# Seven block products instead of eight in the second feed-forward product of a decoder layer

## The chip, the core and the metric

The kernel runs on one core of one Trainium2 chip. The metric is the device time of one execution in microseconds. All operands are float32; matmuls read float32 that has been split into a high and a low part (type fp32r), three matmuls for one product: high x high, low x high, high x low.

## What is computed

The reference is one decoder layer on x of 512 positions and 1024 channels: an input projection into two token mixers, their merge and output projection, a layer norm, and the feed-forward part that the change touches:

```python
h = layer_norm(DEEPNORM_ALPHA * h + mix, ln1_g[l], ln1_b[l])
f = jnp.square(jax.nn.relu(h @ w_ff1[l])) @ w_ff2[l]      # w_ff1 1024 x 4096, w_ff2 4096 x 1024
h = layer_norm(DEEPNORM_ALPHA * h + f, ln2_g[l], ln2_b[l])
```

## The kernel before

The feed-forward part goes through the 4096 hidden channels in four quarters of 1024 (`for q in range(4)`, L890). In each, a first stage (FF1 here) makes the hidden activations of the quarter, and a second stage (FF2) multiplies them by the quarter's 1024 rows of w_ff2 and adds the product to the residual `hn`.

FF1 works on two column blocks n of 512 channels and uses the seven-product form of a 2 x 2 block product (Strassen's, in Winograd's variant): instead of eight products of half-size blocks it makes seven of sums of blocks, numbered p = 1, 2, 5, 6, 3, 7, 4. `ff1_product(n, p)` (L844) runs 24 matmuls of 256 columns with the weight blocks stationary. The sums of the activations (X, L778 to L822, L835) are made once. The sums of the weights are made by DMA: `du_chunks` (L211) loads three chunks for a block: U (two of the four weight blocks, in ring "raw"), V (one) and S (one, twice). `dma_add` (L207) is a DMA on the GpSimd (POOL) queue that adds one tile into another. `s13` (L239) adds U into S, both halves, before product 1 (it is the `pre` of that item); `du_item` (L221) adds S's first half into U's second after product 1's split, for product 6, and U's second half into V after product 2's split, for product 3. FF1's results are kept in small tiles (`small_t`, tag "bt", five buffers, L784), then put through relu and square, and split into `ah` and `al` by `rest` (L880), run behind the next product's matmuls.

FF2 is plain: `b_step` (L726) takes one row block k (128 hidden channels) of w_ff2 and runs 4 position tiles x 2 column halves x 3 matmuls of 512 columns, weights moving, activations stationary, into eight PSUM banks over eight k (L901). Then DVE adds the banks into `hn` (L908). The weights of FF2 come as row pairs (`rows_b`, L168, L263) through ring "raw". In the last quarter the stage is ordered by position tile, so that the last layer norm can start early (L913 to L920).

All weights pass through one `Stream` (L41): a list of chunks (DMA loads into rings of two buffers each, "raw", "V", "S") and a list of items. `ws.get()` returns the split of the next item and prepares the items up to two further on: it issues the loads that a ring has room for (a chunk's place is free when the last item of the chunk two before it has been made) and then the split, `split` (L142): a copy on ScalarE into `whi`, a subtraction on VectorE into `wlo`, three buffers each. Loads are issued by SyncE (SP, L80). `ffseq` (L245) holds the order of the FF1 items: in quarter 0 the two blocks are interleaved by hand, in the others the second block's product 1 comes seventh. The order in which an engine gets its instructions is that of a scheduler that the program goes through, mostly, but not always, the order of the code. `consts` (L719) loads the two vectors of a layer norm into a slab, for the last norm at the end of quarter 0 (L911). "slab" is a pool of eight tiles of 16 KB a partition. `norm_in` and `norm_out` (L739, L745) are the layer norm.

The functions printed below are those that the change touches.

Of the kernel before, what the change touches and what calls it, by code (L numbers as in the profile page):

```python
# [9 lines left out]
F32 = mybir.dt.float32  # L10
F32R = mybir.dt.float32r
# [89 lines left out]
def layer_kernel(ctx: ExitStack, tc: tile.TileContext, x, w_in, gm_ln_g, gm_ln_b, gm_w_s, gm_b_s,  # L101
# [109 lines left out]
    def du_chunks(src, k0, c0):  # L211


        def blk(n, k):
            return src[:, k0 + 4 * k:k0 + 4 * k + 4, c0 + 256 * n:c0 + 256 * n + 256]
        one, two = (lambda t: t[:, 0]), (lambda t: t[:, 1])
        return dict(U=ws.chunk("raw", [2, 4, 256], [(two, blk(0, 0)), (one, blk(1, 1))]),
                    V=ws.chunk("V", [4, 256], [((lambda t: t), blk(0, 1))]),
                    S=ws.chunk("S", [2, 4, 256], [(one, blk(1, 0)), (two, blk(1, 0))]))
# [25 lines left out]
    ffseq = []  # L245
    for q in range(4):
        du = [2 * q, 2 * q + 1]
        if q == 0:
            order = [(0, 1), (0, 2), (1, 1), (1, 2), (0, 5), (0, 6), (0, 3), (0, 7), (1, 5), (0, 4), (1, 6),
                     (1, 3), (1, 7), (1, 4)]  # L250
        else:
            order = [(0, 1), (0, 2), (0, 5), (0, 6), (0, 3), (0, 7), (1, 1), (0, 4), (1, 2), (1, 5), (1, 6),
                     (1, 3), (1, 7), (1, 4)]
        ffseq.append([(2 * q + i, p) for i, p in order])
        dus = {}
        for n, p in ffseq[q]:
            if n not in dus:
                dus[n] = du_chunks(w1v, 0, 512 * n)
# [467 lines left out]
    def b_step(banks, k, hi, lo, ah, al, start, stop, ts, es=(0, 1)):  # L726
        for t in ts:
            ts_ = slice(t * P, (t + 1) * P)
            for e in es:
                cs = slice(e * 512, (e + 1) * 512)  # L730
                ps = banks[2 * t + e]
                nc.tensor.matmul(ps, ah[:, k, ts_], hi[:, cs], start=start, stop=False)  # L732
                nc.tensor.matmul(ps, al[:, k, ts_], hi[:, cs], start=False, stop=False)  # L733
                nc.tensor.matmul(ps, ah[:, k, ts_], lo[:, cs], start=False, stop=stop)  # L734
# [89 lines left out]
    for t in range(4):  # L824
        for e in range(2):
            for k in range(2, 8):
                b_step(ob, k, *last[k - 2], mh, ml, False, k == 7, [t], [e])
# [11 lines left out]
    ah = slab("ah", [P, 8, S], F32R)  # L839
    al = slab("al", [P, 8, S], F32R)  # L840
# [3 lines left out]
    def ff1_product(n, p):  # L844
# [26 lines left out]
        if p == 4:  # L871
            t = small_t("b")
# [4 lines left out]
        c0 = 4 * (n % 2) + (2 if p in (4, 7) else 0)  # L877
        rows, cs = slice(c0, c0 + 2), slice(0, 256) if p in (2, 4) else slice(256, 512)

        def rest():  # L880
            if p != 4:
                nc.scalar.activation(t, t, AF.Relu, scale=-1.0 if p == 7 else 1.0)
            t3 = t.rearrange("p (k i) -> p k i", k=2)
            nc.scalar.activation(t, t, AF.Square)
            nc.scalar.activation(ah[:, rows, cs], t3, AF.Copy)
            nc.vector.tensor_sub(al[:, rows, cs], t3, ah[:, rows, cs].bitcast(F32))

        later.append(rest)

    for q in range(4):  # L890
# [7 lines left out]
        if q == 3:
            res["fh"] = slab("fh", [P, 4, D], F32R)
            res["fl"] = slab("fl", [P, 4, D], F32R)  # L900
        for k in range(8 if q < 3 else 2):  # L901
            hi, lo = ws.get()
            b_step(fb, k, hi, lo, ah, al, k == 0, k == 7, range(4))
        if q < 3:
            for t in range(4):
                for e in range(2):
                    cs = slice(e * 512, (e + 1) * 512)
                    nc.vector.scalar_tensor_tensor(hn[:, t, cs], hn[:, t, cs], ALPHA if q == 0 else 1.0,  # L908
                                                   fb[2 * t + e], op0=ALU.mult, op1=ALU.add)
            if q == 0:  # L910
                consts(ln2_g, ln2_b)  # L911
        else:
            last = [ws.get() for _ in range(6)]  # L913
            for t in range(4):
                for e in range(2):
                    for k in range(2, 8):
                        b_step(fb, k, *last[k - 2], ah, al, False, k == 7, [t], [e])
                    norm_in(t, e, fb, 1.0)
                norm_out(t, EPS, lambda cs: (nc.scalar if cs.start else nc.sync).dma_start(
                    out[t * P:(t + 1) * P, cs], hn[:, t, cs]))  # L920
# [30 lines left out]
```

## Time and profile before

| what | value |
|---|---|
| median of 3 runs | 903.93 us (902.53 to 905.6) |
| profiled execution, its own time | 902.12 us |
| its span, first to last instruction | 900.4 us |
| mean granted TensorE clock | 0.994 |
| busy: PE, DVE, ACT | 883.7, 494.2, 384.4 us |
| DMA | 110.10 MB, mean 122 GB/s |

PE is TensorE, DVE VectorE, ACT ScalarE, POOL GpSimd, SP SyncE, PEld TensorE's weight load, which runs beside the matmuls. A q behind an engine's name is its instruction queue. Busy time is the time in which an engine had an instruction running; matmuls overlap each other in the pipeline. In a table of instructions, "out<-in" names the program's tiles with buffer numbers left out, and "idle" is the time before an instruction in which its engine had nothing running, with what ended it.

### The profile page before, as it was taken

To read this page: it belongs to the slowest core of one execution; us is meant where nothing else is said; L and a number is where in the kernel's file an instruction comes from. 1 tells how busy PE (TensorE), PEld (TensorE's weight loads), DVE (VectorE), ACT (ScalarE), POOL (GpSimd) and SP (SyncE) were. 2 spreads that over 40 slices of the span, in tenths; PEclk is the share of its full clock that TensorE was granted. 3 is DMA by queue.
4 is the path that set the end of the run, shared out by engine and by line. 5 is a ranking of instruction groups with operands and counts; after the bars stand their busy time and mean duration, and the time that the engine had idled before them with its cause. 6 is when DMAs were issued, how large, how long until landed. Compare 5 with 4: busy or idle time off the path is not lost.

```text
span 900.4 us, 12170 instructions
## 1 busy us (share of the span) xinstructions
PE 883.7 (98%) x4864; PEld 762.1 (85%) x4864; DVE 494.2 (55%) x961; ACT 384.4 (43%) x668; POOL 31.0 (3%) x44
## 2 busy tenths in 40 slices
PE   8999999999999999999999998999999999999995
PEld 6888898988888888788788887988998899889984
DVE  3322745542237766667745589742563266346667
ACT  3522312342225566565533316751474167227700
POOL 1000000000000000000000011001100100010000
PEclk9999999999999999999999999899999999999999
DMA  7458510343232011311174653565664866374401
GB/s 233 122 166 244 163 40 25 96 140 94 94 94 77 18 47 48 94 48 48 47 270 152 182 122 71 171 204 140 130 197 141 193 150 188 127 170 110 141 24 70
DMA packets 71513, 110.10 MB, mean 122 GB/s; under 512 B 2656, under 2 KB 54688, under 8 KB 71456
## 3 DMA queue, kind: packets, MB, share of 16 engines
q1 hardware_dynamic: 62336, 85.04, 29.1%
q0 software_dynamic: 4608, 16.78, 9.8%
q10 hardware_dynamic: 4512, 7.50, 2.8%
q8 instruction: 38, 0.62, 0.3%
q14 instruction: 19, 0.16, 0.1%
HBM read 90.44 MB, written 2.10 MB: 103 GB/s over the span
## 4 chain that ended last, share of the span: by engine, by line
PE 97%; DVE 2%; ACT 1%; DMA 0%; issue 0%; DVEq 0%; SPq 0%; ACTq 0%
PE ps L133 13%; PE ps L135 12%; PE ps L134 12%; PE ps L732 8%; PE ps L734 8%; PE ps L733 8%; PE ps L862 6%; PE ps L860 6%; PE ps L863 6%; PE ps L656 2%; PE ps L406 2%; PE ps L407 2%; PE ps L451 2%; PE ps L408 2%; PE ps L671 1%; PE ps L673 1%
## 5 line engine op out<-in xcount | busy, mean ns | idle before, releaser
L151 DVE TENSOR_TENSOR wlo<-raw,whi 128x1024 fp32r<-128x1024 f32 (+3 forms) x131 | 152.8, 1168 | 222.6 <-ACT whi L150 222.4
L150 ACT ACTIVATE whi<-raw 128x1024 fp32r<-128x1024 f32 (+3 forms) x131 | 132.7, 1015 | 270.4 <-PE ps L134 114.9
L860 PE MATMUL ps<-x,whi 128*128 128x256 f32 x448 | 128.5, 287 | 2.9 <-ACT x L800 2.7
L862 PE MATMUL ps<-x,whi 128*128 128x256 f32 x448 | 128.0, 286 | 1.6 <-DVE x L801 1.6
L133 PE MATMUL ps<-xh,whi 128*128 128x512 f32 x320 | 128.8, 403 | 0.0
L863 PE MATMUL ps<-x,wlo 128*128 128x256 f32 x448 | 127.8, 285 | 0.0
L134 PE MATMUL ps<-xl,whi 128*128 128x512 f32 x320 | 125.2, 391 | 0.2 <-DVE xl L338 0.2
L135 PE MATMUL ps<-xh,wlo 128*128 128x512 f32 x320 | 125.2, 391 | 0.0
L860 PEld LDWEIGHTS ps<-x,whi 128*128 128x128 f32 x448 | 87.1, 194 | 5.1 <-ACT x L800 3.3
L862 PEld LDWEIGHTS ps<-x,whi 128*128 128x128 f32 x448 | 87.0, 194 | 2.2 <-DVE x L801 2.1
L732 PE MATMUL ps<-whi,ah 128*128 128x512 f32 x224 | 87.3, 391 | 0.0
L733 PE MATMUL ps<-whi,al 128*128 128x512 f32 x224 | 87.3, 390 | 0.0
L734 PE MATMUL ps<-wlo,ah 128*128 128x512 f32 x224 | 87.2, 389 | 0.0
L863 PEld LDWEIGHTS ps<-x,wlo 128*128 128x128 f32 x448 | 87.0, 194 | 0.0
L135 PEld LDWEIGHTS ps<-xh,wlo 128*128 128x128 f32 x320 | 60.1, 188 | 13.0
L134 PEld LDWEIGHTS ps<-xl,whi 128*128 128x128 f32 x320 | 60.3, 189 | 9.9 <-DVE xl L338 0.5
L133 PEld LDWEIGHTS ps<-xh,whi 128*128 128x128 f32 x320 | 60.2, 188 | 9.3
L615 ACT ACTIVATE PP<-PP,nm 128x512 f32<-128x512 f32 (+3 forms) x64 | 35.8, 559 | 35.5 <-DVE nm L609 35.2
L732 PEld LDWEIGHTS ps<-whi,ah 128*128 128x128 f32 x224 | 42.1, 188 | 9.3 <-ACT b L873 1.0
L734 PEld LDWEIGHTS ps<-wlo,ah 128*128 128x128 f32 x224 | 42.1, 188 | 8.8
L733 PEld LDWEIGHTS ps<-whi,al 128*128 128x128 f32 x224 | 42.1, 188 | 8.4
L660 DVE TENSOR_TENSOR ptl<-ps,pth 128x512 fp32r<-128x512 f32 (+1 forms) x48 | 31.7, 683 | 8.0 <-ACT pth L659 7.9
(205 smaller groups left out, 1529.0 us busy)
## 6 DMA issues: line engine op xcount, KB each, us to landing
raw<-in_w_in_dram SPq DMA_DIRECT2D x17, 1024.0 KB, 5.2
raw<-in_w_ff_dram SPq DMA_DIRECT2D x16, 1024.0 KB, 5.1
S<-in_w_ff_dram SPq DMA_DIRECT2D x16, 512.0 KB, 5.7
raw<-in_w_ff_dram SPq DMA_DIRECT2D x16, 512.0 KB, 4.8
S<-raw POOLq DMA_DIRECT2D x16, 512.0 KB, 5.9
raw<-in_w_in_dram SPq DMA_DIRECT2D x8, 512.0 KB, 3.7
raw<-in_w_proj_gm_dram SPq DMA_DIRECT2D x4, 1024.0 KB, 5.2
raw<-in_w_proj_nsa_dram SPq DMA_DIRECT2D x4, 1024.0 KB, 5.1
```

Of the source, the lines that this page charges most:

```text
L133: nc.tensor.matmul(ps, hi, mh, start=start, stop=False)
L134: nc.tensor.matmul(ps, hi, ml, start=False, stop=False)
L135: nc.tensor.matmul(ps, lo, mh, start=False, stop=stop)
L150: nc.scalar.activation(hi, r, AF.Copy)
L151: nc.vector.tensor_sub(lo, r, hi.bitcast(F32))
L615: nc.scalar.activation(t, t, AF.Exp, bias=nm[:, e, i:i + 1], scale=-1.0, accum_out=sm[:, e, i:i + 1])
L732: nc.tensor.matmul(ps, ah[:, k, ts_], hi[:, cs], start=start, stop=False)
L733: nc.tensor.matmul(ps, al[:, k, ts_], hi[:, cs], start=False, stop=False)
L734: nc.tensor.matmul(ps, ah[:, k, ts_], lo[:, cs], start=False, stop=stop)
L860: nc.tensor.matmul(o, hi[:, k, js], xh[:, k], start=opens and j == 0 and k == 0, stop=False, skip_group_check=True)
L862: nc.tensor.matmul(o, hi[:, k, js], xl[:, k], start=False, stop=False, skip_group_check=True)
L863: nc.tensor.matmul(o, lo[:, k, js], xh[:, k], start=False, stop=j == 1 and k == 3, skip_group_check=True)
```

## The change

In quarters 0 to 2, FF2 also uses the seven-product form. Its 2 x 2 blocks are: position halves of 256, hidden-channel halves of 512, and output-column halves of 512. The weight blocks are loaded and summed by the same three chunks and DMA adds (`ff2_blocks`, a quarter has two sets h, each half of the hidden channels of a block). The sums of the activations (Y) are made in `rest`, from the small tiles, by subtractions on VectorE, and split into new slabs y12, y56, y37 and the free half of x4; `ah` and `al` go. `ff2_product` runs, for each p in the order 1, 2, 6, 5, 7, 3, 4 and each of the two sets, 2 x 2 x 3 matmuls of 512 columns, weights moving; products that add into one output share their banks, and after each product VectorE adds or subtracts two banks into `hn`. Quarter 3 keeps the plain form, with the activations taken from Y1, Y2, Y5 and Y3. The load of the last norm's vectors moves to quarter 3. The "bt" ring has six buffers instead of five.

The core of the diff (`b_step` now asks a function for its activation tiles, which is left out here, as are the changed calls):

```diff
+    def ff2_blocks(q, h):
+        def blk(half, k):
+            k0 = 8 * q + 4 * k + 2 * h
+            return w2v[:, k0:k0 + 2, 512 * half:512 * half + 512]
+        return du_chunks([2, 512], blk)
...
-    ffseq = []
+    ffseq, FF2 = [], (1, 2, 6, 5, 7, 3, 4)
...
         if q < 3:
-            rows_b(w2v, list(range(8 * q, 8 * q + 8)), 0, 1024)
+            dus = [ff2_blocks(q, h) for h in range(2)]
+            for p in FF2:
+                for h in range(2):
+                    du_item(dus[h], p, s13(dus[h]) if p == 1 else None)
...
-    ah = slab("ah", [P, 8, S], F32R)
-    al = slab("al", [P, 8, S], F32R)
+    y12 = slab("y12", [P, 4, D], F32R)
+    y56 = slab("y56", [P, 4, D], F32R)
+    y37 = slab("y37", [P, 4, D], F32R)
+    Y = {p: (block(t, i), block(t, i + 1)) for p, (t, i) in
+         {1: (y12, 0), 2: (y12, 2), 5: (y56, 0), 6: (y56, 2), 3: (y37, 0), 7: (y37, 2), 4: (x4, 2)}.items()}
...
+        def y_split(c, t):
+            t3 = t.rearrange("p (k i) -> p k i", k=2)
+            nc.scalar.activation(Y[c][0][:, rows], t3, AF.Copy)
+            nc.vector.tensor_sub(Y[c][1][:, rows], t3, Y[c][0][:, rows].bitcast(F32))
 
         def rest():
             if p != 4:
                 nc.scalar.activation(t, t, AF.Relu, scale=-1.0 if p == 7 else 1.0)
-            t3 = t.rearrange("p (k i) -> p k i", k=2)
             nc.scalar.activation(t, t, AF.Square)
-            nc.scalar.activation(ah[:, rows, cs], t3, AF.Copy)
-            nc.vector.tensor_sub(al[:, rows, cs], t3, ah[:, rows, cs].bitcast(F32))
+            t11, t12, t22 = g[1], g.get(6), g.get(5)
+            plain = n // 2 == 3
+            if p == 2:
+                y_split(1, t)
+            elif p == 3:
+                if plain:
+                    y_split(5, t)
+                else:
+                    nc.vector.tensor_sub(t11, t11, t12)
+                    y_split(5, t11)
+            elif p == 7:
+                y_split(3, t)
+                if not plain:
+                    nc.vector.scalar_tensor_tensor(t11, t11, -1.0, t22, op0=ALU.mult, op1=ALU.subtract)
+                    y_split(6, t11)
+                    nc.vector.tensor_sub(t12, t22, t12)
+                    y_split(7, t12)
+            else:
+                y_split(2, t)
+                if not plain:
+                    nc.vector.scalar_tensor_tensor(t, t11, -1.0, t, op0=ALU.mult, op1=ALU.subtract)
+                    y_split(4, t)
...
+    def ff2_product(q, p):
+
+        where = {1: "A", 2: "B", 5: "C", 6: "A", 3: "C", 7: "A", 4: "A"}[p]
+        opens = p in (1, 2, 5)
+        if opens:
+            g2[where] = [bank(t) for t in {"A": "dd", "B": "aa", "C": "ac"}[where]]
+        for h in range(2):
+            hi, lo = ws.get()
+            for j in range(2):
+                js = slice(j * P, (j + 1) * P)
+                ps = g2[where][j]
+                for kk in range(2):
+                    yh, yl = (y[:, 2 * h + kk, js] for y in Y[p])
+                    nc.tensor.matmul(ps, yh, hi[:, kk], start=opens and h == 0 and kk == 0, stop=False,
+                                     skip_group_check=True)
+                    nc.tensor.matmul(ps, yl, hi[:, kk], start=False, stop=False, skip_group_check=True)
+                    nc.tensor.matmul(ps, yh, lo[:, kk], start=False, stop=h == 1 and kk == 1,
+                                     skip_group_check=True)
+        half, e, sign, first = {1: (0, 0, 1, 1), 2: (0, 0, 1, 0), 6: (1, 0, 1, 1), 5: (1, 1, -1, 1),
+                                7: (1, 1, -1, 0), 3: (1, 0, 1, 0), 4: (0, 1, -1, 1)}[p]
+        for j in range(2):
+            v = hn[:, 2 * half + j, e * 512:(e + 1) * 512]
+            nc.vector.scalar_tensor_tensor(v, v, ALPHA if q == 0 and first else 1.0, g2[where][j],
+                                           op0=ALU.mult, op1=ALU.add if sign > 0 else ALU.subtract)
...
+        if q < 3:
+            for p in FF2:
+                ff2_product(q, p)
+            continue
         fb = eight()
...
+        consts(ln2_g, ln2_b)
```

## Rows read from the trace of the kernel before

**Rows 1.** The page, part 4: the chain that ended last, by engine.

```profile
PE 97%; DVE 2%; ACT 1%; DMA 0%; issue 0%; DVEq 0%; SPq 0%; ACTq 0%
```

**Rows 2.** Windows: start:end, length, busy us (x instructions), clock, DMA share, GB/s.

```profile
core 0: us, PE busy (x) PEld busy (x) DVE busy (x) ACT busy (x) POOL busy (x), PEclk, DMA share, GB/s
593.20:636.50 43.30, 43.30 (x202) 36.12 (x203) 13.55 (x14) 12.04 (x14) 4.26 (x5) 1.00 0.59 152
636.50:677.40 40.90, 40.90 (x329) 40.00 (x327) 27.24 (x32) 28.19 (x39) 2.55 (x3) 1.00 0.61 169
```

**Rows 3.** Timeline of PE inside FF2: start us, duration us, instruction.

```profile
604.47 0.39 PE L732 MATMUL ps<-whi,ah 128*128 128x512 f32 x1
...
630.31 0.39 PE L732 MATMUL ps<-whi,ah 128*128 128x512 f32 x1
```

**Rows 4.** Groups by line and shape, window 593.2 to 677.4.

```profile
L151 DVE TENSOR_TENSOR wlo<-raw,whi 128x1024 fp32r<-128x1024 f32 x15 | 18.4, 1224 | 28.1 <-ACT whi L150 28.1
L150 ACT ACTIVATE whi<-raw 128x1024 fp32r<-128x1024 f32 x14 | 14.8, 1060 | 30.9 <-PE ps L733 23.2 <-PE ps L862 7.7
...
L908 DVE SCALAR_TENSOR_TENSOR hn<-hn,ps 128x512 f32<-128x512 f32 x8 | 5.0, 679 | 4.0 <-PE ps L734 4.0
```

**Rows 5.** Windows at the start of FF1 in quarter 0.

```profile
550.00:555.00 5.00, 5.00 (x44) 5.00 (x43) 4.96 (x13) 3.83 (x6) 0.26 (x1) 1.00 0.56 108
560.00:565.00 5.00, 2.08 (x8) 1.78 (x9) 5.00 (x9) 3.28 (x6) 0.00 (x0) 0.68 0.00 0
565.00:570.00 5.00, 5.00 (x30) 5.00 (x30) 4.62 (x7) 2.03 (x3) 0.00 (x0) 0.64 0.61 213
```

**Rows 6.** Timeline of PE there.

```profile
559.08 0.28 PE L863 MATMUL ps<-x,wlo 128*128 128x256 f32 x1
...
563.50 0.58 PE L862 MATMUL ps<-x,whi 128*128 128x256 f32 x1 [0.82 <-DVE x L801]
```

**Rows 7.** Waits of SP's queue: us in total, times, longest.

```profile
SPq L721 <- DVE T L820: 52.3, 1, 52.3
```

**Rows 8.** Timeline of DVE: the last two splits of w2 (rows 30, 31).

```profile
856.31 2.36 DVE L151 TENSOR_TENSOR wlo<-raw,whi 128x1024 fp32r<-128x1024 f32 x2 [0.35 <-ACT whi L150]
```

**Rows 9.** Line L732 on the kept w2 rows of quarter 3: ns min/median/max, first and last start.

```profile
L732 PE MATMUL ps<-fh,ah x32: 389/389/389, 858.5 to 889.1; 128*128 128x512 f32 x32
```

**Rows 10.** Timeline of SP's queue: the issue of one U, two halves.

```profile
613.59 0.93 SPq L80 DMA_DIRECT2D raw<-in_w_ff_dram  x2
```

**Rows 11.** Timeline of POOL: issues of DMA adds; in brackets idle time before, its end.

```profile
549.00 0.84 POOL L208 DMA_DIRECT2D raw<-S  x1 [2.44 <-DVE rs L315]
554.74 0.85 POOL L208 DMA_DIRECT2D V<-raw  x1 [4.90 <-DVE hn L764]
...
619.19 0.86 POOL L208 DMA_DIRECT2D S<-raw  x1 [0.57 <-DMA raw<-in_w_ff_dram]
...
630.61 1.12 POOL L208 DMA_DIRECT2D raw<-S  x1
640.60 0.85 POOL L208 DMA_DIRECT2D V<-raw  x1 [8.88 <-DMA raw<-S]
652.67 0.84 POOL L208 DMA_DIRECT2D raw<-S  x1 [11.21 <-DVE wlo L151]
660.64 0.86 POOL L208 DMA_DIRECT2D V<-raw  x1 [7.12 <-DMA raw<-S]
```

**Rows 12.** Timeline of ACT: the split of V that waited for its add.

```profile
665.33 1.06 ACT L150 ACTIVATE whi<-V 128x1024 fp32r<-128x1024 f32 x1 [0.88 <-DMA V<-raw]
```

**Rows 13.** DMA view, window 590 to 690; issues: KB each, median us to landing.

```profile
DMA packets 8377, 16.48 MB, mean 165 GB/s; under 512 B 398, under 2 KB 5694, under 8 KB 8371
...
S<-raw POOLq DMA_DIRECT2D x4, 512.0 KB, 5.2
```

**Rows 14.** The chain that ended last in order of time: start, us.

```profile
592.49 0.23 PE ps L732
593.18 0.33 PE ps L860
```

**Rows 15.** A window with an add and loads together.

```profile
652.00:657.00 5.00, 5.00 (x44) 5.00 (x43) 3.40 (x5) 3.88 (x5) 0.84 (x1) 1.00 1.04 288
```

More of the change, by code (lines that the diff above doesn't have):

```diff
@@ L209, in dma_add, with du_chunks, ff1_blocks, blk @@
                             accum_op=ALU.add)
-    def du_chunks(src, k0, c0):
-        def blk(n, k):
-            return src[:, k0 + 4 * k:k0 + 4 * k + 4, c0 + 256 * n:c0 + 256 * n + 256]
+    def du_chunks(shape, blk):
         one, two = (lambda t: t[:, 0]), (lambda t: t[:, 1])
-        return dict(U=ws.chunk("raw", [2, 4, 256], [(two, blk(0, 0)), (one, blk(1, 1))]),
-                    V=ws.chunk("V", [4, 256], [((lambda t: t), blk(0, 1))]),
-                    S=ws.chunk("S", [2, 4, 256], [(one, blk(1, 0)), (two, blk(1, 0))]))
+        return dict(U=ws.chunk("raw", [2] + shape, [(two, blk(0, 0)), (one, blk(1, 1))]),
+                    V=ws.chunk("V", shape, [((lambda t: t), blk(0, 1))]),
+                    S=ws.chunk("S", [2] + shape, [(one, blk(1, 0)), (two, blk(1, 0))]))
+    def ff1_blocks(n):
+        def blk(half, k):
+            c0 = 1024 * (n // 2) + 512 * half + 256 * (n % 2)
+            return w1v[:, 4 * k:4 * k + 4, c0:c0 + 256]
+        return du_chunks([4, 256], blk)
+    def ff2_blocks(q, h):
+        def blk(half, k):
+            k0 = 8 * q + 4 * k + 2 * h
+            return w2v[:, k0:k0 + 2, 512 * half:512 * half + 512]
+        return du_chunks([2, 512], blk)
     def du_item(d, p, pre=None):
@@ L724, in layer_kernel, with b_step @@
     consts(ln1_g, ln1_b)
-    def b_step(banks, k, hi, lo, ah, al, start, stop, ts, es=(0, 1)):
+    def b_step(banks, k, hi, lo, get, start, stop, ts, es=(0, 1)):
         for t in ts:
-            ts_ = slice(t * P, (t + 1) * P)
+            th, tl = get(k, t)
             for e in es:
@@ L731, in b_step @@
                 ps = banks[2 * t + e]
-                nc.tensor.matmul(ps, ah[:, k, ts_], hi[:, cs], start=start, stop=False)
-                nc.tensor.matmul(ps, al[:, k, ts_], hi[:, cs], start=False, stop=False)
-                nc.tensor.matmul(ps, ah[:, k, ts_], lo[:, cs], start=False, stop=stop)
+                nc.tensor.matmul(ps, th, hi[:, cs], start=start, stop=False)
+                nc.tensor.matmul(ps, tl, hi[:, cs], start=False, stop=False)
+                nc.tensor.matmul(ps, th, lo[:, cs], start=False, stop=stop)
     def eight():
@@ L767, in norm_out, with m_tile @@
                     emit(cs)
+    def m_tile(k, t):
+        return mh[:, k, t * P:(t + 1) * P], ml[:, k, t * P:(t + 1) * P]
     ob = eight()
@@ L771, in layer_kernel @@
         hi, lo = ws.get()
-        b_step(ob, k, hi, lo, mh, ml, k == 0, False, range(4))
+        b_step(ob, k, hi, lo, m_tile, k == 0, False, range(4))
     last = [ws.get() for _ in range(6)]
@@ L826, in layer_kernel @@
             for k in range(2, 8):
-                b_step(ob, k, *last[k - 2], mh, ml, False, k == 7, [t], [e])
+                b_step(ob, k, *last[k - 2], m_tile, False, k == 7, [t], [e])
             norm_in(t, e, ob, 2.0 * ALPHA)
@@ L890, in layer_kernel, with a_tile @@
+    def a_tile(k, t):
+        y = Y[{(0, 0): 1, (1, 0): 2, (0, 1): 5, (1, 1): 3}[k // 4, t // 2]]
+        ts_ = slice(t % 2 * P, t % 2 * P + P)
+        return y[0][:, k % 4, ts_], y[1][:, k % 4, ts_]
     for q in range(4):
@@ L896, in layer_kernel @@
             later.pop(0)()
+        if q < 3:
+            for p in FF2:
+                ff2_product(q, p)
+            continue
         fb = eight()
[L898 to L920, printed above, removed]
+        res["fh"] = slab("fh", [P, 4, D], F32R)
+        res["fl"] = slab("fl", [P, 4, D], F32R)
+        consts(ln2_g, ln2_b)
+        for k in range(2):
+            b_step(fb, k, *ws.get(), a_tile, k == 0, False, range(4))
+        last = [ws.get() for _ in range(6)]
+        for t in range(4):
+            for e in range(2):
+                for k in range(2, 8):
+                    b_step(fb, k, *last[k - 2], a_tile, False, k == 7, [t], [e])
+                norm_in(t, e, fb, 1.0)
+            norm_out(t, EPS, lambda cs: (nc.scalar if cs.start else nc.sync).dma_start(
+                out[t * P:(t + 1) * P, cs], hn[:, t, cs]))
 _INS = ['x', 'w_in', 'gm_ln_g', 'gm_ln_b', 'gm_w_s', 'gm_b_s', 'cmp_pe_k', 'cmp_w1_k', 'cmp_w2_k',
```

10 lines of the change are left out of this document (5 added, 5 removed).

## The prediction

> **What bounds the kernel now.** First the page's chain: TensorE (PE) carries 97% of what ended last [rows 1]. So the time is the sum of PE's instructions, and an edit is worth the PE time it removes, less the new time in which PE waits. The table of windows cuts the changed part into stages: a second-product stage ("FF2") of 43.3 us, then a first-product stage ("FF1") of 40.9 us, PE busy all through both, VectorE (DVE) and ScalarE (ACT) at about a third in FF2 and two thirds in FF1, the DMA engines at 0.6 [rows 2]. Last the timelines: a matmul's duration (0.39 us) overlaps the next one, so its price is the step from start to start. Between the two starts shown lie 114 matmuls of 512 columns in 25.84 us: 0.2267 us each [rows 3]. FF1 and FF2 of a quarter take 84.2 us [rows 2]; the 192 FF2 matmuls are 43.5, so 336 FF1 matmuls share 40.7: 0.121 us each, and one FF1 item (24 matmuls) is 2.91 us.
>
> **What is removed.** FF2 of a quarter had 8 x 4 x 2 x 3 = 192 matmuls. Afterwards it has 7 products x 2 halves x 2 row tiles x 2 k x 3 = 168, of the same shape (stationary 128x128 activations, 512 weight columns moving), so the same step holds. Three quarters lose 24 each: 72 x 0.2267 = 16.3 us. That is the whole possible gain: 902.1 (the profiled execution; its span is 900.4) becomes 885.8. The median of the runs, 903.9, lies 1.8 above the profiled one, and I add that at the end.
>
> **Work beside PE.** An FF2 quarter gets 14 weight splits instead of 8 (1.06 us ACT, 1.22 DVE) and 14 bank drains instead of 8 (0.68 DVE) [rows 4]: DVE 26.6 us and ACT 14.8 us, beside 168 x 0.2267 = 38.1 us of PE. Hidden. FF1 of quarters 0 to 2 gets, for its two blocks, 14 activation splits instead of 8 and 8 combinations: 6 copies on ACT, each half as wide as a weight split's 1.06, and 14 DVE instructions of the drain's shape (0.68) [rows 4]. On the windows' times: ACT at most 28.2 + 6.4 = 34.6, DVE 27.2 + 9.5 = 36.7 of 40.9 us [rows 2]. Hidden, but DVE stands at 90%. The nearest rows for a full DVE are the start of FF1 in quarter 0, where DVE was busy in 4.96 to 5.00 of 5.00 us and PE had one matmul between 559.08 and 563.50, 4.4 us [rows 5, 6]. Bounds 0 to 4.4 us a quarter; I take 0, since 10% is left and whi/wlo have three buffers, so that a split may be nearly two items late. A gain is excluded: nothing is taken from these engines.
>
> The drains don't hold PE: products 1, 6, 7, 4 share banks, and between each two lies another product of 5.4 us against 2 x 0.68 of draining. Y of product 1 comes early in FF1, and Y2, the last of the first ones, is wanted 5.4 us after FF2 begins. y37, a ninth slab, can reuse hraw, free before product 7. The sixth bt buffer only adds room.
>
> The constants move from quarter 0 to quarter 3. Before, SP (the queue that issues loads) stood 52.3 us with them at its head, weight loads behind [rows 7]; no PE wait follows from it, so freeing it gains 0. In quarter 3 their two issues wait for a slab that FF1's last products free, and their 1 MB passes ahead of the last w2 rows. The nearest price is U's 1 MB, 5.6 us from issue to landing (below). Those rows are split by 856.31 + 2.36 = 858.7 [rows 8], while the row-26 matmuls begin at 858.5 and rows 30 and 31 come 12 matmuls (2.7 us) later [rows 9]: 2.5 us to spare. 0 taken, as the loads overlap; up to 3.1 in the range.
>
> **The chain that decides.** A new set of weight blocks needs DMAs in a row: U loads; S += U; U1 += S0 (for product 6); V += U1 (for product 3). Before, w2 rows lay between two FF1 stages, used unchanged, and gave this chain time. Now every item uses it. Prices: U, issued at 613.59, lets its second S add go at 619.19, 5.6 later [rows 10, 11]; an S add lands in 5.2 [rows 13]. U1 += S0, from its issue to the start of the V add that waits for it, takes at most 5.7 us (549.00 to 554.74), 8.0 beside S loads (652.67 to 660.64), and 10.0 with two other adds ahead (630.61 to 640.60) [rows 11]; the V add 4.7, to the split at 665.33 [rows 12]. After landing, a split costs some 2.0 us before PE can run through.
>
> *Entering FF1 after FF2* (0 = its first matmul). The raw buffer is freed by the split of product 4, half 0, which starts four items of 2.72 ahead, at -10.9, and ends near -8.4. U: -2.8; product 1 is in time. S0: +2.4. U1: +8.1 to +12.4, so product 6 can run from 10.1 to 14.4. The written order wants it as fourth item, at 8.7. But the order on PE is not the written one: in the chain an FF2 matmul (L732, 592.49) stands ahead of the last FF1 product (L860, 593.18) [rows 14]. The program is ordered by readiness, so I expect products 1 and 2 of the second block, whose U and V are there, to go ahead of product 6: it is then wanted at 14.5, not late. Product 3 is wanted at 17.4 and has V at 12.8 to 17.1, split at 14.8 to 19.1. Late by 0 to 1.7 us; I take 1.7, the row with two adds ahead, since the second block's S adds fall here. Three times: 5.1 us.
>
> *Entering FF2.* U of half 1 is freed by the split of the last FF1 product, starting at -8.7: S0 at +4.5, U1 at +10.2 to +14.5, product 6 of half 1 ready at 12.2 to 16.5, wanted as sixth item at 13.6. Late 0 to 2.9; with 8.0 us, the row beside S loads, 0.9. Three times: 2.7 us.
>
> **Sum:** 16.3 - 5.1 - 2.7 = 8.5 us; 902.1 - 8.5 = 893.6, and with 1.8 **895.4**.
>
> How far can these latencies be trusted? 100 us of the trace move 16.48 MB [rows 13], a quarter 13.9. Eight further adds of 0.52 MB and 1.05 MB more loads make 19.1 MB in 79 us. The window with an add and loads together moved 288 GB/s [rows 15], at which this is 66 us: 84% of the quarter, so queues will form. The Trainium skill (Trainium Kernel Development and Optimization, Key Constraints) says that DMAs from the SP, ACT and POOL queues run on the same 16 engines and interleave; the trace agrees, with 5.7 us for raw<-S against 8.0 beside S loads [rows 11].
>
> **Rivals.** *Everything hides* (more reordering, adds of 5.7): the full 16.3, 887.6. For it: FF1 runs the same chain now without a PE wait, and 5.7 makes each wait zero. Against: the DMA engines carry nearly 40% more.
>
> *The written order stays*, and PE waits for product 6 and then product 3 at each FF1: the slower side. With 5.7 us product 6 is 1.4 late and product 3 1.8 after it, 3.2 a quarter; with 8.0 it is 3.7 + 1.8 = 5.5, and 0.9 on entering FF2. Three times 6.4 is 19.2, and the gain is gone: it decides from about 8 us for U1 += S0. The gap of 4.4 us also took PE's granted clock to a mean of 0.68 and 0.64 in the next windows: 36 matmuls from 563.50 to 570.00 took 6.5 us instead of 4.4 [rows 5, 6]. With these 2.1, 8.5 a quarter, 25.5 - 16.3 = 9.2 slower: 913.1. For it: rows 14 show a few matmuls moved, not whole items. Against: that anything moves by readiness.
>
> *The adds starve.* POOL issues them (0.84 us each) while DVE is at 90%. If each of the three chained adds waited for one DVE instruction of 1.22 us, six entrances would lose 3.7 each, 22 us: 909.8. Against: where DVE was busy 4.96 of 5.00 us, raw<-S at 549.00 still took 0.84 to issue, and the add behind it started at 554.74 [rows 5, 11]. The Trainium skill (SBUF — State Buffer, SBUF: two separate sides) states that POOL cannot write a DMA's descriptors while DVE runs a 2-port mode; by its figures (about 620 ns alone, 3100 beside a copy) each add would gain some 2.5 us, an estimate, and the chain 7.4. The two-input DVE instructions here show nothing of it [rows 11].
>
> That the code runs other counts than said is excluded; that the new matmuls step slower than 0.2267 would need another operand layout, and there is none.
>
> **How the numbers follow.** Forecast 0.45, everything hides 0.25, written order 0.20, starved adds 0.05, a full DVE or late w2 rows (the forecast plus 3 to 13) 0.05. A measurement here tells 0.3%, 2.7 us, from no change. The first two are faster by more; the written order with short adds and the mildest of the last end near no change. Faster 0.68, same 0.10, slower 0.22. Range 887 to 912: from the full gain to near the middle of the written-order case.
>
> **What would show it.** Right: a quarter period near 82 us instead of 84.2, FF2 near 38 to 39, and PE idle of 1 to 2 us before FF1 and FF2 items, ended by splits that waited for DMA raw<-S or V<-raw. Wrong: gaps of 4 us and a granted clock under 1 after each FF2 (written order); DVE without pauses in FF1 and splits late by DVE (crowding); POOL's adds over 1 us to issue (starved). If no wait appears at all, the time is 888.

## The result, and the profile after

The changed kernel takes 928.82 us (median of 4 runs, 923.77 to 930.41), beside 904.0 us for the kernel before in the same session: a ratio of 1.0265 [1.0221, 1.0308]. It is slower by 2.7%, and the time lies above the whole predicted range. Run times below are medians as well; one slow execution, of e9 and 3061.2 us long, is left out. The profiled execution took 929.51 us, its span is 927.8 us, and its mean granted clock is 0.983, where 0.994 was read before.

The page says first that the work did get less: 4792 matmuls instead of 4864, the 72 that were to go. PE is now idle for 5% of the span. The chain that ended last answers to [rows 1]; it was followed back for only a tenth of the span here, so its shares are no measure of the whole, but a DMA stands in it now.

```profile
PE 884.8 (95%) x4792; PEld 759.1 (82%) x4792; DVE 550.9 (59%) x1039; ACT 408.7 (44%) x704; POOL 51.3 (6%) x68
...
PE 8%; issue 1%; DMA 1%; DVE 1%; ACT 0%; DVEq 0%; ACTq 0%; POOLq 0%
```

Then the windows, in the columns of [rows 2], cut where a first product starts and where its 13th of 14 products ends (the 14th stands among the first matmuls of FF2, so it is counted there). They are FF2 of quarter 0, FF1 and FF2 of quarter 1, FF1 of quarter 2, and two windows inside FF1 of quarter 1.

```profile
594.30:640.00 45.70, 42.77 (x194) 33.89 (x193) 31.96 (x39) 21.03 (x25) 6.81 (x8) 1.00 0.83 222
640.00:690.00 50.00, 41.92 (x314) 40.66 (x314) 27.85 (x33) 27.40 (x39) 7.04 (x9) 0.93 0.79 188
690.00:732.80 42.80, 41.92 (x193) 34.04 (x193) 31.95 (x39) 21.12 (x25) 6.93 (x9) 1.00 0.85 225
732.80:780.80 48.00, 41.99 (x313) 40.72 (x313) 27.71 (x33) 27.41 (x39) 6.57 (x9) 0.93 0.81 194
645.00:655.00 10.00, 5.84 (x32) 5.22 (x31) 1.23 (x1) 2.10 (x3) 0.96 (x2) 0.83 0.71 138
655.00:665.00 10.00, 8.08 (x51) 7.68 (x52) 5.64 (x6) 6.37 (x10) 0.73 (x1) 0.83 0.44 106
```

Cut the same way, the kernel before had 37.4 us for FF1 and 46.8 for FF2. So FF2 gained: 45.7 in quarter 0, 42.9 in each of the next two. FF1 lost far more: 49.9, 48.0 and 48.3 us in quarters 1 to 3. The account against the span of before: 2.8 us are already lost where the feed-forward part starts, ahead of everything that was changed (unexplained); FF1 costs 12.5 + 10.6 + 10.9 = 34.0; FF2 gives 1.1 + 3.9 + 4.0 = 9.0. That is 27.8, beside 27.4 between the spans.

Where FF1 waits is seen in PE's timeline. These are its five waits in the first half of FF1 of quarter 1. Four stand at the first use of a split: the first two in product 5 (S0), the next two in product 6 (U1). The fifth, in product 3, waits for a bank that ScalarE (L888) has still to drain:

```profile
648.23 0.39 PE L879 MATMUL ps<-x,whi 128*128 128x256 f32 x1 [2.28 <-ACT whi L150]
649.49 0.48 PE L882 MATMUL ps<-x,wlo 128*128 128x256 f32 x1 [0.75 <-DVE wlo L151]
655.55 0.38 PE L879 MATMUL ps<-x,whi 128*128 128x256 f32 x1 [1.68 <-ACT whi L150]
656.81 0.58 PE L882 MATMUL ps<-x,wlo 128*128 128x256 f32 x1 [0.76 <-DVE wlo L151]
661.65 0.39 PE L879 MATMUL ps<-x,whi 128*128 128x256 f32 x1 [0.60 <-ACT b L888]
```

PE waits for ScalarE, but ScalarE is no bottleneck: its own timeline shows what it waited for, and POOL's shows when the adds were issued (the columns of [rows 11, 12]).

```profile
636.31 1.06 ACT L150 ACTIVATE whi<-raw 128x1024 fp32r<-128x1024 f32 x1 [3.40 <-DMA raw<-in_w_ff_dram]
...
647.12 1.06 ACT L150 ACTIVATE whi<-S 128x1024 fp32r<-128x1024 f32 x1 [8.76 <-DMA S<-raw]
...
654.44 1.06 ACT L150 ACTIVATE whi<-raw 128x1024 fp32r<-128x1024 f32 x1 [5.78 <-DMA raw<-S]
659.53 1.06 ACT L150 ACTIVATE whi<-V 128x1024 fp32r<-128x1024 f32 x1 [1.51 <-DMA V<-raw]
```

```profile
636.76 0.84 POOL L208 DMA_DIRECT2D S<-raw  x1 [22.00 <-DMA raw<-in_w_ff_dram]
638.48 0.85 POOL L208 DMA_DIRECT2D S<-raw  x1 [0.87 <-DMA raw<-in_w_ff_dram]
640.07 0.84 POOL L208 DMA_DIRECT2D S<-raw  x1 [0.74 <-DVE wlo L151]
641.18 0.85 POOL L208 DMA_DIRECT2D S<-raw  x1 [0.27 <-DMA raw<-in_w_ff_dram]
647.58 0.84 POOL L208 DMA_DIRECT2D raw<-S  x1 [5.54 <-DMA S<-raw]
654.88 0.85 POOL L208 DMA_DIRECT2D V<-raw  x1 [6.46 <-issue]
```

So the chain S, U1, V runs link by link, and PE behind it. With FF1 starting at 640.04, and by the starts of the splits, U's first half has landed at -3.7, S0 at +7.1, U1 at +14.4, V at +19.5. Four S adds, two for each block, are in flight together ahead of U1 += S0. The first of them is S1 += U1: it goes as soon as the half of U has landed that product 1's split also reads. S0 += U0 is the second; the other half of U lets it go at 638.48, at -1.6. The U loads that open the chain were issued at -8.6; before, SP issued them from 613.59 on, 24.9 us ahead of FF1 [rows 10].

The DMA view of the same 100 us as [rows 13] shows the price. An S add, 5.2 us before, now has a median of 8.1:

```profile
q0 software_dynamic: 2374, 8.61, 46.0%
q1 hardware_dynamic: 8804, 12.05, 35.5%
...
S<-raw POOLq DMA_DIRECT2D x8, 512.0 KB, 8.1
raw<-S POOLq DMA_DIRECT2D x5, 512.0 KB, 6.8
V<-raw POOLq DMA_DIRECT2D x4, 512.0 KB, 5.4
```

Two more windows of the same execution tell the links apart, one with the four S adds in flight, one with one add at a time. A third lies between PE's first waits (the share counts all packets that begin in a window, so it can pass 1):

```profile
636.00:647.00 11.00, 9.95 (x67) 9.04 (x65) 3.56 (x4) 2.04 (x2) 3.39 (x4) 1.00 1.08 255
647.00:655.00 8.00, 4.89 (x24) 4.48 (x24) 1.23 (x1) 2.10 (x3) 0.96 (x2) 0.79 0.62 120
650.00:653.00 3.00, 3.00 (x16) 3.00 (x16) 0.00 (x0) 0.00 (x0) 0.00 (x0) 0.50 0.63 120
```

While the S adds fly, the DMA engines have no room left (1.08), which the stage's mean of 0.79 hides. Behind them they have (0.62): there the links take their own time, one after the other.

### The profile page after: what moved, and what is told of

It reads as the page before. It is cut to its first block, busy times and chain, and to the rows that moved or that the text cites. A ratio compares the mean times of both kernels' runs of the same rounds, so it can differ in the third digit from the quotient of the medians.

```text
span 927.8 us, 12312 instructions
## 1 busy us (share of the span) xinstructions
PE 884.8 (95%) x4792; PEld 759.1 (82%) x4792; DVE 550.9 (59%) x1039; ACT 408.7 (44%) x704; POOL 51.3 (6%) x68
## 5 line engine op out<-in xcount | busy, mean ns | idle before, releaser
L151 DVE TENSOR_TENSOR wlo<-raw,whi 128x1024 fp32r<-128x1024 f32 (+3 forms) x125 | 145.2, 1165 | 184.9 <-ACT whi L150 184.2
L150 ACT ACTIVATE whi<-raw 128x1024 fp32r<-128x1024 f32 (+3 forms) x125 | 126.1, 1012 | 239.5 <-PE ps L134 115.4
L879 PE MATMUL ps<-x,whi 128*128 128x256 f32 x448 | 133.7, 299 | 18.3 <-ACT whi L150 10.1
L881 PE MATMUL ps<-x,whi 128*128 128x256 f32 x448 | 131.7, 294 | 1.6 <-DVE x L817 1.6
L879 PEld LDWEIGHTS ps<-x,whi 128*128 128x128 f32 x448 | 90.9, 203 | 22.5 <-ACT whi L150 11.4
L881 PEld LDWEIGHTS ps<-x,whi 128*128 128x128 f32 x448 | 90.9, 203 | 2.2 <-DVE x L817 2.1
L950 PE MATMUL ps<-wlo,y 128*128 128x512 f32 x144 | 56.9, 395 | 3.3 <-DVE wlo L151 3.3
L947 PE MATMUL ps<-whi,y 128*128 128x512 f32 x144 | 56.7, 394 | 1.4 <-ACT whi L150 1.4
L949 PE MATMUL ps<-whi,y 128*128 128x512 f32 x144 | 56.2, 390 | 0.0
L208 POOL DMA_DIRECT2D S<-raw x28 | 24.3, 890 | 568.9 <-DMA raw<-in_w_ff_dram 539.7
L151 DVE TENSOR_TENSOR wlo<-S,whi 128x1024 fp32r<-128x1024 f32 x28 | 34.0, 1222 | 25.0 <-ACT whi L150 24.9
L151 DVE TENSOR_TENSOR wlo<-V,whi 128x1024 fp32r<-128x1024 f32 x28 | 34.2, 1223 | 21.4 <-ACT whi L150 20.5
L150 ACT ACTIVATE whi<-S 128x1024 fp32r<-128x1024 f32 x28 | 29.3, 1055 | 36.6 <-DMA S<-raw 15.8
```

Of the source, the lines that this page charges most:

```text
L150: nc.scalar.activation(hi, r, AF.Copy)
L151: nc.vector.tensor_sub(lo, r, hi.bitcast(F32))
L879: nc.tensor.matmul(o, hi[:, k, js], xh[:, k], start=opens and j == 0 and k == 0, stop=False, skip_group_check=True)
L881: nc.tensor.matmul(o, hi[:, k, js], xl[:, k], start=False, stop=False, skip_group_check=True)
L947: nc.tensor.matmul(ps, yh, hi[:, kk], start=opens and h == 0 and kk == 0, stop=False, skip_group_check=True)
L949: nc.tensor.matmul(ps, yl, hi[:, kk], start=False, stop=False, skip_group_check=True)
```

## Experiments

### Is it the adds? e2_noadds, e3_nocomb

e2_noadds leaves out the DMA adds of FF1 in quarters 1 to 3; the weight blocks are loaded and split, but not summed:

```diff
-                du_item(dus[n], p, s13(dus[n]))
+                du_item(dus[n], p, s13(dus[n]) if q == 0 else None, q == 0)
```

> Leaves out all DMA adds of the first products in quarters 1 to 3 (so the weight sums of those quarters are not made). If the chain of adds is the cause, FF1 comes back to about 37.4 us in each, 34 us less in all: 892 to 897, under the kernel before. If VectorE and ScalarE are the cause, the time stays above 920.

Measured: 892.19 us, ratio 0.9865 [0.9849, 0.9881]. The windows of quarter 1 (its FF1 with the 14th product, then the rest of FF2) and of the whole of quarter 2:

```profile
639.40:680.60 41.20, 41.20 (x340) 40.80 (x339) 30.98 (x37) 30.72 (x44) 4.04 (x5) 1.00 0.57 166
680.60:718.60 38.00, 37.71 (x168) 30.83 (x167) 28.57 (x34) 18.10 (x22) 2.77 (x4) 1.00 0.80 207
718.60:798.00 79.40, 78.88 (x505) 71.54 (x504) 58.87 (x70) 48.77 (x64) 6.82 (x8) 1.00 0.67 186
```

FF1 is at its old 37.4 us, PE busy throughout, and a quarter takes 79.2 and 79.4 us where the full gain would make it 84.2 - 5.4 = 78.8. All that FF1 lost hangs on the adds (the run is 36.6 us under the changed kernel), and the 16.3 us of matmuls are there to be had. It doesn't say what about the adds costs the time, their bytes or their order; the next runs ask that.

e3_nocomb leaves out the combinations on VectorE (the products then read uncombined activations):

```diff
-                    nc.vector.tensor_sub(t11, t11, t12)
...
-                    nc.vector.scalar_tensor_tensor(t11, t11, -1.0, t22, op0=ALU.mult, op1=ALU.subtract)
...
-                    nc.vector.tensor_sub(t12, t22, t12)
...
-                    nc.vector.scalar_tensor_tensor(t, t11, -1.0, t, op0=ALU.mult, op1=ALU.subtract)
```

> Leaves out the four VectorE combinations of the activations per block in quarters 0 to 2 (24 instructions of 0.69 us). If the DMA chain is the cause, the time changes by less than 4 us: 924 to 930. If a full VectorE is, it falls by 10 us or more, to 918 or less.

Measured: 928.82 us, 1.0276 [1.0248, 1.0304], FF1 of quarter 1 at 46.2 us, with most of that lost again in its FF2 (45.9). The time does not move: the combinations' load on VectorE is not the cause.

### Is it the order? e1_order, e4_sorder, e8_both

e1_order gives quarters 1 to 3 the order of quarter 0, where the second block's products 1 and 2 stand ahead of the first block's product 5:

```diff
-        if q == 0:
+        if True:
```

> Only the listed order of the first-product items in quarters 1 to 3 changes, to the one of quarter 0 (products 1 and 2 of the second block third and fourth). If the waits come from the chain of DMA adds that a block's products 5, 6 and 3 wait for, FF1 of these quarters falls from 48 to 50 us to 40 to 43 and the time to 905 to 912. If the DMA engines' throughput or full VectorE and ScalarE queues set it, nothing is won by an order: 922 or more.

Measured: 926.42 us, 1.0242 [1.0225, 1.0259]. FF1 fell by only some 4 us in quarter 1 and 3 in quarter 2, and rose in quarter 3. Instead of several short waits PE has one long one in each quarter, 18.7 us in three, up to 9.2. The waits view of PE, and ScalarE's timeline at the one of quarter 1:

```profile
PE ps L879 <- ACT b L888: 18.7, 3, 9.2
```

```profile
659.84 1.06 ACT L150 ACTIVATE whi<-V 128x1024 fp32r<-128x1024 f32 x1 [4.32 <-DMA V<-raw]
...
663.59 0.57 ACT L888 ACTIVATE b<-ps 128x512 f32<-128x512 f32 x1
```

L888 drains a bank of a product that PE had long finished. It is ready, but it stands in ScalarE's queue behind a split whose V has not landed. PE then waits for the bank. A late add thus holds not only the product that needs it, but all that is queued behind its split.

e4_sorder holds the second block's two S adds back until the first block's V add has been issued:

```diff
+            with tc.issue_after(state["vadd"].ins) if late else ExitStack():
+                for i in range(2):
+                    dma_add(d["S"]["tile"][:, i], d["U"]["tile"][:, i])
```

> Only the order on the GpSimd queue changes: in quarters 1 to 3 the second block's two S adds go behind the first block's whole chain instead of ahead of its U add. If four S adds at once are what made the first block's S late (10 us instead of 5), FF1 of quarters 1 to 3 falls by 3 to 5 us each, 914 to 920, unless the second block is late in its turn (924 to 932, with the waits moved to its products 5, 6 and 3). If they were not, 926 to 930 with the waits where they are.

Measured: 924.44 us, 1.0219 [1.0182, 1.0255], FF1 at 47.3, 47.5 and 49.0 us. The first block's links get shorter (S0 lands 5.7 us after FF1's start instead of 7.1), so the second block's two adds account for 1.4 us of S0's lateness and no more. The second block does not become the late one: in each quarter all PE waits of FF1 still lie in its first 21 us. Of e4's waits on PE from 590 to 880 us, the largest group is again a drain that stands on ScalarE behind V's split:

```profile
PE ps L880 <- ACT b L889: 9.3, 3, 3.5
```

e8_both does both:

> Quarter 0's order of items in quarters 1 to 3 and, with it, the second block's S adds behind the first block's chain. If the first block's chain alone is what counts, its S comes 3 to 5 us sooner and products 6 and 3 are wanted 6 us later: 905 to 912. If the second block's chain, started later, is then the late one, or bank drains queue behind late splits on ScalarE as in the run with the order alone, 918 to 928.

Measured: 923.83 us, 1.0212 [1.0185, 1.0239]. Neither order is the cure. That the drains should go ahead of the late splits on ScalarE, or to another engine, was not tried.

### Can the chain start sooner? e7_earlyu, e9_earlyu2

Both free U earlier, by taking product 4's weights in FF2 from elsewhere (so that product is another one than the reference's): e7_earlyu from V, e9_earlyu2 from a slab that is always there.

```diff
-               4: lambda: u(0)}[p]
+               4: (lambda: res["x12"][:, 0].bitcast(F32).rearrange("p (k c) -> p k c", k=2)) if early
+               else lambda: u(0)}[p]
```

> Product 4 of the second products in quarters 0 to 2 takes the V block instead of the second U block (so that product is of other data): the U buffers are then free after product 6, eight items earlier, and the next block's chain can start some 20 us sooner. Every load, add, split and matmul stays, and so does the DMA traffic. If the late start of the chain is the cause, FF1 of quarters 1 to 3 comes back to 38 to 41 us and the time to 892 to 903. If the throughput of the DMA engines or of the add queue is, it stays at 918 or more.

> As the run with V in product 4, but product 4's weight item now reads a tile that is always there (so that product is of other data): U is free after product 6, and V and S as in the changed kernel. Loads, adds, splits and matmuls are the same in number and bytes. If the chain's late start is the cause, FF1 of quarters 1 to 3 is 37.5 to 40 us, 892 to 900. If DMA throughput is, 912 or more.

Measured: e7 914.72 us, 1.0119 [1.0087, 1.0151]; there V, now held longer, loads late, and one wait of some 5 us a quarter takes the place of the others, so this run doesn't separate the theories. e9: 917.64 us, 1.0152 [1.0124, 1.018], FF1 at 45.2 to 46.2 us. POOL's timeline in e9; the DMA view of the second S add alone (window 630.2 to 630.6); the window of the four S adds; and the largest group of PE's waits:

```profile
628.84 0.84 POOL L208 DMA_DIRECT2D S<-raw  x1 [13.91 <-DMA S<-in_w_ff_dram]
630.32 0.86 POOL L208 DMA_DIRECT2D S<-raw  x1 [0.64 <-DMA S<-in_w_ff_dram]
...
640.42 0.84 POOL L208 DMA_DIRECT2D raw<-S  x1 [6.22 <-DVE hn L957]
```

```profile
S<-raw POOLq DMA_DIRECT2D x1, 512.0 KB, 9.5
```

```profile
628.00:640.00 12.00, 12.00 (x55) 9.93 (x54) 8.59 (x10) 4.25 (x4) 3.40 (x4) 1.00 1.09 284
```

```profile
PE ps L880 <- ACT b L889: 14.3, 6, 4.2
```

S0's add is issued 11 us before FF1 starts at 640.18, yet U1 += S0 goes only at 640.42. It must wait for both S adds, and S1's, issued at 630.32, takes 9.5 us and lands at 639.8. The other things that it follows cost 0.6 us at most: product 1's split, which waits on ScalarE for PE to free a buffer and begins at 634.71 (VectorE's half ends at 637.04), and a drain on VectorE. Before, U1 += S0 went 7.9 us ahead of FF1 [rows 11]. The S adds wait for the load of S now, not for U, and the loads of S and V fly beside them: the engines are as full (1.09) as they were later in the changed kernel. By the run's own expectation, 912 or more speaks for DMA throughput, and for this stretch the windows agree. What PE waits for longest is, as in e1, drains that stand on ScalarE behind a late split. Starting U sooner gives back some 11 us and no more.

### Which engine should add? e5_pooladd, e6_dveadd, e11_dveorder, e10_all

e5_pooladd replaces every DMA add by an add on GpSimd itself:

```diff
-        nc.gpsimd.dma_start(dst.rearrange("p k c -> p (k c)"), src.rearrange("p k c -> p (k c)"),
-                            accum_op=ALU.add)
+        dst, src = (t.rearrange("p k c -> p (k c)") for t in (dst, src))
+        nc.gpsimd.tensor_add(dst, dst, src)
```

> All sums of weight blocks are made by GpSimd instructions from SBUF to SBUF instead of DMAs that add. If one takes about 2 us, the chain of three links is 6 to 8 us instead of 25 to 28, and everything hides: 886 to 895. If GpSimd takes 5 us or more for one (56 of them in a row), or holds up VectorE, the chain is as long as before: 910 to 935.

Measured: 964.14 us, 1.0668 [1.0649, 1.0687]. GpSimd's group of S adds (window 590 to 890), and two of VectorE's groups in FF1 of quarter 1:

```profile
L209 POOL TENSOR_TENSOR S<-S,raw 128x1024 f32<-128x1024 f32 x24 | 72.2, 3026 | 101.3 <-DMA raw<-in_w_ff_dram 77.2 <-DVE hn L956 24.1
```

```profile
L151 DVE TENSOR_TENSOR wlo<-raw,whi 128x1024 fp32r<-128x1024 f32 x7 | 12.8, 1828 | 1.1 <-ACT whi L150 1.1
...
L895 DVE TENSOR_TENSOR b<-b,ps 128x512 f32<-128x512 f32 x6 | 4.1, 682 | 3.7 <-PE ps L882 3.7
```

The time is above both ranges of the expectation. An add takes 3.0 us, well under a DMA's 8.1, but VectorE's low split goes from 1223 ns (the same group after the change) to 1828 on average, and VectorE is busy for 47.0 of the 58.8 us of FF1 with its 14th product. No single wait explains the whole loss.

e6_dveadd puts two of the links, U1 += S0 and V += U1 of FF1 in quarters 1 to 3, on VectorE, in the code behind product 5's split:

```diff
-            if p == 1:
+            if p == 1 and not dve:
...
-            if p == 2:
+            if p == 2 and not dve:
...
+            if p == 5 and dve:
+                nc.vector.tensor_add(u(1), u(1), s(0))
+                nc.vector.tensor_add(v(), v(), u(1))
```

> U += S0 and V += U of the first products in quarters 1 to 3 are made by VectorE, behind product 5's split, instead of by DMA; the S adds stay on DMA. If the chain's length is the cause, two links of 5 to 8 us become 1.2 us each; the S adds remain, so product 5 may still wait 2 to 3 us: FF1 39 to 43 us, 900 to 910. If VectorE at 90 percent is close to a bound, the 24 more instructions of 1.2 us give 10 us back and more: 910 to 920.

Measured: 910.75 us, 1.0084 [1.0067, 1.0101]; FF1 40.9, 41.7 and 40.9 us. Two links of 7 and 5 us become two instructions of 1.22, and 18 of the 25 us come back. What is left in FF1 are three short waits a quarter, 2.7 us together in quarter 1, all behind S. The scheduler sets U1 += S0 ahead of the low half of product 5's split, and there it waits for the S add:

```profile
642.89 1.23 DVE L246 TENSOR_TENSOR raw<-raw,S 128x1024 f32<-128x1024 f32 x1 [5.37 <-DMA S<-raw]
```

e11_dveorder adds the order of e1, and e10_all also lets the first two products of FF2 alternate between the two sets:

> VectorE makes U += S0 and V += U in FF1 of quarters 1 to 3, and the items have quarter 0's order there, so that product 5 is wanted 6 us later. If what was left with the VectorE sums alone (FF1 41 us) is the wait for S, FF1 falls to 38 to 39 and the time to 898 to 904. If it is VectorE's load, it stays at 908 to 913.

> The same, and in FF2 the items of products 1 and 2 alternate between the halves, so that half 1's U, which comes late, is wanted one item (2.7 us) later. If the wait at FF2's start is that load, each FF2 of quarters 0 to 2 loses 1 to 2.5 us: 892 to 900, below the kernel before. If not, as the run without it.

Measured: 913.97 us, 1.0112 [1.0074, 1.0149], and 917.34 us, 1.0147 [1.0114, 1.018]. e10 is worse than e6; e11 is no better (the intervals overlap). In e11 VectorE stands where ScalarE stood in e1, with the add that waits for a DMA at the head of its queue and splits behind it:

```profile
643.98 1.23 DVE L246 TENSOR_TENSOR raw<-raw,S 128x1024 f32<-128x1024 f32 x1 [5.18 <-DMA S<-raw]
```

### Which links are left? e12_s0dve, e13_ff2dve

e12_s0dve takes the first block's S0 += U0 to VectorE as well. e13_ff2dve does the same as e12, and in FF2 too puts U1 += S0 and V += U1 on VectorE, ahead of product 6's split:

```diff
+            if p == 6 and dve == 2:
+                nc.vector.tensor_add(u(1), u(1), s(0))
+                nc.vector.tensor_add(v(), v(), u(1))
             out = split(src())
+            if p == 1 and lead:
+                nc.vector.tensor_add(s(0), s(0), u(0))
...
-                    du_item(dus[h], p, s13(dus[h]) if p == 1 else None)
+                    du_item(dus[h], p, s13(dus[h]) if p == 1 else None, 2)
```

> As e6 (U1 += S0 and V += U1 on VectorE in the first product of quarters 1 to 3), and the first block's S0 += U0 as well, behind the split of product 1; only S1 of that block still goes by DMA. Theory (the last link that holds PE in e6 is S0's DMA add, which lands some 9 us after its issue because four S adds and a U load share the engines): the split of product 5 no longer waits for a DMA, the first products of quarters 1 to 3 take 37.4 to 38 us instead of 40.9, 41.8 and 41.0, and the time falls by about 10 us from e6's 910.75, to 898 to 903. Rival A (VectorE is full: 32 us busy in e6, 33.4 of 37.4 here): the low splits come late instead, the stages stay at 40 us or more, and the time is 907 to 911. Rival B (the wait only moves, to S1 at product 7 or to the second block's adds): one gap a quarter behind product 3, 904 to 909.

> As e12, and in the second product too U1 += S0 and V += U1 run on VectorE, ahead of product 6's split, so that only the S adds are left to the DMA queue there. Theory (what the second product still loses, 42.9 to 44 us against 38.1 us of matmuls, is raw<-S landing late for product 6): the stages of quarters 1 and 2 take 40 to 41.5 us, the time is 4 to 8 us under e12's, about 894, and both kernels are beaten. Rival (VectorE is the limit: 30 us busy of 40 before, 35 with four more instructions of 1.2 us, and in order): its stages stay at 43 us or more, low splits late by DVE, and the time is e12's or up to 5 us over it.

Measured: e12 910.62 us, 1.0068 [1.0047, 1.0089], no better than e6 and not what the theory said. VectorE's and POOL's timelines of e12:

```profile
639.82 1.22 DVE L245 TENSOR_TENSOR S<-S,raw 128x1024 f32<-128x1024 f32 x1
644.12 1.23 DVE L251 TENSOR_TENSOR raw<-raw,S 128x1024 f32<-128x1024 f32 x1 [3.09 <-DMA S<-raw]
645.27 1.22 DVE L151 TENSOR_TENSOR wlo<-V,whi 128x1024 fp32r<-128x1024 f32 x1
```

```profile
638.03 0.84 POOL L208 DMA_DIRECT2D S<-raw  x1 [23.41 <-DMA raw<-in_w_ff_dram]
```

S0 is done at 641.04, and U1 += S0 still waits for an S add by DMA. The only one of this block is S1 += U1, issued at 638.03. It reads U1, which the next add overwrites. The chain thus had a link that neither the prediction nor the expectation of e12 had: U1 += S0 must wait for both S adds, for one because it reads the sum and for the other because that one still reads U1. And U1 += S0 waits at the head of VectorE's queue, ahead of product 2's low split (645.27), for which PE then waits 3.4 us in quarter 1 and 1.9 and 1.6 in the next two.

e13: 897.2 us (896.56 to 897.96, 5 runs), 0.9926 [0.9912, 0.994]. It beats both kernels, 7.0 us under the one before. FF1 takes 37.4 us in quarter 1, 37.5 in quarter 2 and 38.7 in quarter 3, where e12 took 42.5, 41.0 and 39.5. The windows of FF2 of quarter 1 (cut as after the change), in e12 and in e13:

```profile
682.40:726.00 43.60, 41.88 (x194) 34.09 (x193) 31.70 (x38) 20.89 (x25) 6.31 (x8) 1.00 0.85 224
```

```profile
674.00:718.40 44.40, 42.39 (x194) 33.95 (x193) 35.38 (x42) 20.90 (x25) 2.55 (x3) 1.00 0.57 170
```

The share of the DMA engines falls from 0.85 to 0.57, but FF2 gets no shorter: the 40 to 41.5 us of the expectation did not come. The gain came in FF1, whose code is the same in both. VectorE's timeline of e13 there:

```profile
635.99 1.22 DVE L151 TENSOR_TENSOR wlo<-V,whi 128x1024 fp32r<-128x1024 f32 x1
...
638.32 1.22 DVE L151 TENSOR_TENSOR wlo<-S,whi 128x1024 fp32r<-128x1024 f32 x1
639.45 1.22 DVE L251 TENSOR_TENSOR raw<-raw,S 128x1024 f32<-128x1024 f32 x1
```

The scheduler here set U1 += S0 behind the low splits of products 2 and 5, where e12 has it ahead of both. When its turn comes in quarters 1 and 2 the S add has landed, and PE waits for nothing in FF1; in quarter 3 the add still waits 1.6 us. U's landing doesn't explain the difference: product 1's split starts 4.0 us ahead of FF1 in quarter 1 of e13, but 3.9 us ahead in quarter 2 of e12, which still lost 3.6 us. FF1 gives 9.4 of the 11.8 us between the two profiled spans, and the edit did not ask for this order, so much of its gain is luck. e12 with this order was not tried, and why the scheduler chose it stays open.

## Why the prediction was wrong

- **What is removed** was right: 72 matmuls fewer at the same step. With the adds out of FF1 (e2) a quarter gains 4.8 to 5.0 of the 5.4 us.
- **Work beside PE** was right: no price for VectorE's combinations (e3), and none seen for the moved constants. FF2 of quarter 3 takes 46.4 us, as before.
- **Entering FF1** was wrong: 12.5, 10.6 and 10.9 us where 1.7 a quarter was forecast. The start of the chain was nearly right (U issued at -8.4, measured -8.6; landed at -2.8, where S0's add, which needs U's second half, measured -1.6). Three terms behind it failed.
  - *S0 at +2.4*: measured +7.1. Of the 4.7 us, 1.2 are the later go; the rest is the add itself, 8.6 us to the split behind it. The price of 5.2 us came from a stretch in which S adds go in pairs, 9.7 us apart; here four start within 4.5 us, as the two blocks' U are freed by two neighbouring items, and the DMA engines are full. The prediction set the second block's adds beside U1 only, where they had in fact begun ahead of it; e4 gives them 1.4 us of the 3.4. S0 alone thus made product 5 late (the first two waits, 3.0 us), for which no step and no rival had a wait. And U1 also waits for S1, which no step had; in the changed kernel that is free, as S1's add is issued and lands first, but it held e9 and e12.
  - *"The program is ordered by readiness, so I expect products 1 and 2 of the second block to go ahead of product 6"*: they did not. PE ran the products of quarters 1 to 3 in the written order. Six FF2 matmuls ahead of the last FF1 product (one of them in [rows 14]) were taken for a rule that moves whole items. And e1, which writes that order, shows that it would have saved little: splits and drains queue behind the late split.
  - *The clock*, for which the sum had nothing: each wait is short, but PE's granted clock falls to 0.83 in the two windows of 10 us shown, as it had to 0.68 and 0.64 behind the gap of [rows 5]. From 650 to 653 us it is 0.50, its lower level of 1.2 GHz, and matmuls of 256 columns step 0.21 us there instead of 0.12. The listed waits sum to 6.1 us, and one of 2.0 behind ScalarE's drain follows near the end of the stage. The other 4.4 of the 12.5 us are matmuls at the lower clock, some 3.1 us by their steps, and the first matmuls behind each wait.
- **Entering FF2**: 0.9 us a quarter was forecast; quarters 1 and 2 lose 1.5 and 1.4 of 5.4, quarter 0 loses 4.3, of which 2.9 are PE's waits for splits. Why quarter 0 loses more stays open.
- **The rivals.** *The written order stays* had the right order, the waits in product 6 and product 3 and the clock, with a chance of 0.20, and was still too mild: 8.5 us a quarter and 913.1, for it used the same S0 and so had no wait in product 5. *The adds starve* falls: in this part POOL issues them in 0.84 to 0.87 us, but for three of 1.19 that follow straight on another. (The row of [rows 5] that the prediction sets against it begins at 550, behind the add of 549.00.) *Everything hides* was the furthest off.

The prediction's worry, 84% of the DMA engines' room, came out at shares of 0.79 to 0.85 in the stage windows. But the sum put no price on it, and the mean hid the stretch that counts: the S adds fly at 1.08. The two links behind them take 6.9 and 4.7 us to the splits that wait for them, at a share of 0.62: there the engines have room, and it is the time of one link after the other that counts. The Trainium skill (Trainium Kernel Development and Optimization, Key Constraints) says that the queues' transfers run on the same 16 engines and interleave. The runs agree: the S add takes 5.2, 8.1 or, with fewer adds around it in e13, 5.8 us in the median.

Open: why a quarter of e13 still takes 81.8 and 82.6 us where e2 takes 79.2 and 79.4. FF1 is the same within 0.1 us, so the rest lies in FF2. The largest group in PE's waits view of e13, from 590 to 880 us, is now the low splits of FF2 on VectorE, whose queue holds the adds:

```profile
PE ps L959 <- DVE wlo L151: 5.7, 7, 1.7
```

That is some 2 of the 3 us a quarter; what holds the rest was not tried.

## What to carry to other kernels

A change that takes work off the bound engine also takes away the time in which other chains hid: draw up the whole chain, with what still reads each buffer that is summed in place, against the order that the code writes, and price each link at the number of transfers that will be in flight then, from a window that holds those transfers and not from the mean of a stage. An engine's queue runs in order: an instruction that waits for a late DMA holds all that stands behind it (ScalarE in e1, where PE waited up to 9.2 us, and in e9; VectorE in e11 and e12). A short add that gates others belongs on an engine with a fixed duration, placed behind what is ready; the DMA queue suits those adds whose result is wanted much later.

## What the runs showed of the hardware

- **An accumulating DMA is dear.** In the 100 us shown after the change the adds' queue (q0) moved 8.61 MB in 46.0% of the engines' time, 5.3% per MB; the loads (q1) 12.05 MB in 35.5%, 2.9% per MB.
- **GpSimd's adds slow VectorE selectively** (e5): subtractions of two SBUF tiles went from 1223 to 1828 ns, while the add whose second input lies in PSUM stayed at 682 (681 after the change). The Trainium skill (SBUF — State Buffer, SBUF: two separate sides) says that a VectorE instruction with two SBUF inputs and a GpSimd instruction that reads SBUF exclude each other; the two groups agree with it.
